# Half of the first feed-forward product by seven block products instead of eight

## The chip, the cores and the metric

The kernel runs on one core of a Trainium2 chip. The metric is the time that the device needs for one execution, in microseconds (us); the lower the better. The engines named here are TensorE (PE, matrix products; PEld is its weight load), VectorE (DVE), ScalarE (ACT), GpSimd (POOL) and SyncE (SP, which issues the loads). SBUF is the core's working memory, PSUM the eight banks of 128 x 512 fp32 into which PE adds up its products.

## The reference, cut to what matters

One encoder block on 256 tokens of width 2048, all in float32: a mixer of two branches (retention and latent attention), gated and merged, and then a feed-forward part of width 8192. The change touches the latter only:

```python
D_MODEL = 2048; SEQ = 256; D_FF = 4 * D_MODEL

h = h + _mixer(u, positions, ...)                # ends in  merged @ w_out
z = _rmsnorm(h, norm_mlp_g[l]) @ w_up[l]         # (256 x 2048) @ (2048 x 8192)
h = h + jnp.square(jax.nn.relu(z)) @ w_down[l]   # (256 x 8192) @ (8192 x 2048)
return _rmsnorm(h, norm_f_g)
```

## The kernel before

**Split products.** Every large product is made of fp32r products: an operand is split into `hi`, its value cast to fp32r, and `lo`, the rest, and `hi*hi + hi*lo + lo*hi` is summed in PSUM. `weights` (L146 to L153) does that for a weight tile: SP loads 512 KB into a `raw` buffer (L148), ACT casts it to `hi` (L151), DVE subtracts to get `lo` (L152). There are five `raw` buffers and four each of `hi` and `lo`. `split` (L214 on) does the same to activations. Since a weight is used for all 256 tokens only, each of them is loaded, split and used once, and the loads run all through the kernel.

**First product.** hT is the transposed and normalized h, kept as hi and lo in SBUF. `w_up` is cut into 64 units of 128 columns. A unit (`t_unit`, L170) loads and splits two half-weights of 128x1024, then PE runs 16 matmuls with a block of `hi` stationary and 512 columns moving, hi and lo of hT side by side (`t_pass1`, L159), and 16 with a block of `lo` stationary and the 256 columns of hT's hi (`t_pass2`, L163). `joined` (L204 to L212) adds the two halves of the bank: ACT copies one (L206), DVE adds (L207, tile `val`). DVE squares what is above zero into `hid` (L800), which stays in SBUF. The units take turns in the four PSUM banks of the pool behind `mmps`; the other four (`atps`) serve transposes here. The first two units are begun in halves, since the last quarter of hT (`mlp_turn(3)`) is transposed after their first half.

**Before and after it.** The w_out product (L770 to L779) ends the mixer, and `mlp_turn` (L757) makes hT of its result, a quarter at a time. The second product (`down`, L807, lines L814 to L816) has hid's halves stationary and 512 columns of w_down moving, in all eight PSUM banks, and the kernel ends in normalizing and storing the output.

**What sets the order.** All engines have queues of their own and work in order. The program is written in order of the data, and the framework's scheduler then orders each engine's instructions by a simulated timeline; the first loads and the last two units of the second product are held to the written order.

## Time and profile before

| what | value |
|---|---|
| median of 3 runs | 1631.94 us (1631.42 to 1632.12) |
| profiled execution | 1632.22 us, its span 1630.4 us |
| first product, from its first matmul to the first of the second product | 915.47 to 1272.66 us, 357.2 us |
| granted PE clock, mean | 0.998 |
| HBM read / written | 300.84 MB / 2.10 MB |

The profile comes from one execution. Busy time of an engine is what its instructions cover; PE's matmuls overlap, so their price is read from the distance of their starts, not from the duration given. "A <- B" in a wait means that A stood idle until B was done. Lines (L152) are those of the kernel before. Groups by line tell the name of the tile written, then those read: `lo<-raw,hi`, `z<-hT,hi`. Where a window is asked for (915:1273, in us from the start of the span), busy times are those inside it.

### The profile page before, as it was taken

The page shows a single profiled execution, that of the slowest core. Times are in us where ns is not written, and L with a number is a line of the kernel's source. Part 1 is how long each engine was busy: PE and PEld are TensorE (multiplying, and loading weights), DVE is VectorE, ACT ScalarE, POOL GpSimd, SP SyncE. Part 2 cuts the span into 40 slices and gives each one's busy share as a digit, 9 for nine tenths or more (in the row PEclk, how much of TensorE's full clock was granted, in tenths as well). Part 3 has the DMA queues.
Part 4 walks back from the last instruction along what each step waited for, and adds up shares of the span by engine and source line. Part 5 has one row for each costly group of instructions (what it writes and reads, how often), then busy time and mean ns, then how long its engine had stood idle before and what let it go on. Part 6 is the DMA issues. An engine that isn't in the chain of part 4 may idle for free.

```text
span 1630.4 us, 23041 instructions
## 1 busy us (share of the span) xinstructions
PE 1614.9 (99%) x8782; PEld 1398.8 (86%) x8782; DVE 996.2 (61%) x1491; ACT 809.7 (50%) x1249; POOL 49.5 (3%) x62
## 2 busy tenths in 40 slices
PE   8999999999999999999999999999999999999997
PEld 6888888888889889888888888888888888888886
DVE  7974588655556658666765555555555555555555
ACT  6544555544445556765545544444444444444444
POOL 7100000000000000000000000000000000000001
PEclk9999999999999999999999999999999999999999
DMA  8665544555556554325575555555555655555553
GB/s 306 200 233 193 187 156 166 169 192 186 190 170 203 190 191 146 125 94 176 186 246 187 174 193 188 192 189 186 191 192 184 223 194 192 193 193 195 192 194 112
DMA packets 84480, 304.46 MB, mean 187 GB/s; under 512 B 9360, under 2 KB 9488, under 8 KB 83600
## 3 DMA queue, kind: packets, MB, share of 16 engines
q1 hardware_dynamic: 84368, 302.98, 55.3%
q8 instruction: 69, 1.13, 0.3%
q14 instruction: 43, 0.35, 0.1%
HBM read 300.84 MB, written 2.10 MB: 186 GB/s over the span
## 4 chain that ended last, share of the span: by engine, by line
PE 97%; DVE 1%; issue 0%; DMA 0%; ACT 0%; POOL 0%; SPq 0%; DVEq 0%; POOLq 0%; ACTq 0%
PE z L159 14%; PE z L163 8%; PE dn L816 7%; PE dn L814 7%; PE dn L815 7%; PE rg L159 4%; PE yr L159 4%; PE gr L159 4%; PE gm L159 4%; PE mo L159 4%; PE qk L159 2%; PE gr L163 2%; PE yr L163 2%; PE gm L163 2%; PE rg L163 2%; PE mo L163 2%
## 5 line engine op out<-in xcount | busy, mean ns | idle before, releaser
L152 DVE TENSOR_TENSOR lo<-raw,hi 128x1024 fp32r<-128x1024 f32 (+2 forms) x562 | 666.0, 1204 | 521.6 <-ACT hi L151 248.3
L151 ACT CAST hi<-raw 128x1024 fp32r<-128x1024 f32 (+2 forms) x562 | 580.8, 1035 | 536.9 <-PE z L159 135.2
L159 PE MATMUL z<-hT,hi 128*128 128x512 f32 x1024 | 245.5, 391 | 0.0
L159 PEld LDWEIGHTS z<-hT,hi 128*128 128x128 f32 x1024 | 188.0, 188 | 36.1
L815 PE MATMUL dn<-lo,dh 128*128 128x512 f32 x512 | 199.2, 389 | 0.0
L816 PE MATMUL dn<-hi,dl 128*128 128x512 f32 x512 | 199.2, 389 | 0.0
L814 PE MATMUL dn<-hi,dh 128*128 128x512 f32 x512 | 198.9, 389 | 0.0
L163 PEld LDWEIGHTS z<-hT,lo 128*128 128x128 f32 x1024 | 131.6, 191 | 5.1
L163 PE MATMUL z<-hT,lo 128*128 128x256 f32 x1024 | 133.1, 283 | 0.0
L815 PEld LDWEIGHTS dn<-lo,dh 128*128 128x128 f32 x512 | 96.1, 188 | 20.1
L816 PEld LDWEIGHTS dn<-hi,dl 128*128 128x128 f32 x512 | 96.1, 188 | 19.9
L814 PEld LDWEIGHTS dn<-hi,dh 128*128 128x128 f32 x512 | 96.1, 188 | 19.8
L216 ACT CAST dh<-hid 128x256 fp32r<-128x256 f32 x64 | 26.0, 407 | 89.3 <-PE dn L815 89.3
L159 PE MATMUL mo<-my,hi 128*128 128x512 f32 x256 | 65.5, 396 | 0.4 <-DVE val L207 0.4
L159 PE MATMUL rg<-x,hi 128*128 128x512 f32 x256 | 64.0, 395 | 0.0
L159 PE MATMUL yr<-ry,hi 128*128 128x512 f32 x256 | 61.4, 391 | 0.0
L159 PE MATMUL gr<-x,hi 128*128 128x512 f32 x256 | 61.3, 391 | 0.0
L159 PE MATMUL gm<-x,hi 128*128 128x512 f32 x256 | 61.1, 391 | 0.0
L159 PEld LDWEIGHTS gm<-x,hi 128*128 128x128 f32 x256 | 47.0, 188 | 9.1
L159 PEld LDWEIGHTS gr<-x,hi 128*128 128x128 f32 x256 | 47.0, 188 | 9.0
L159 PEld LDWEIGHTS yr<-ry,hi 128*128 128x128 f32 x256 | 46.9, 188 | 9.0
L159 PEld LDWEIGHTS rg<-x,hi 128*128 128x128 f32 x256 | 46.2, 188 | 8.6
(271 smaller groups left out, 2239.1 us busy)
## 6 DMA issues: line engine op xcount, KB each, us to landing
raw<-w_up SPq DMA_DIRECT2D x128, 512.0 KB, 4.2
raw<-w_down SPq DMA_DIRECT2D x128, 512.0 KB, 4.3
raw<-w_rv SPq DMA_DIRECT2D x32, 512.0 KB, 4.5
raw<-w_rg SPq DMA_DIRECT2D x32, 512.0 KB, 4.5
raw<-w_gret SPq DMA_DIRECT2D x32, 512.0 KB, 4.3
raw<-w_ret_o SPq DMA_DIRECT2D x32, 512.0 KB, 4.6
raw<-w_gmla SPq DMA_DIRECT2D x32, 512.0 KB, 4.4
raw<-w_out SPq DMA_DIRECT2D x32, 512.0 KB, 3.7
```

Source lines behind the costliest of these rows:

```text
L151: SC.copy(hi, raw)
L152: V.tensor_tensor(out=lo, in0=raw, in1=hi.bitcast(F32), op=ALU.subtract)
L159: PE.matmul(out, w[0][:, k], x.both(k0 + k), start=start and k == 0, stop=False)
L163: PE.matmul(out[:, :S], w[1][:, k], x.hi(k0 + k), start=False, stop=stop and k == n - 1)
L216: SC.copy(hi, val)
L814: mm(PE.matmul(out, dh[:, ts], hi[:, ws], start=i == 0, stop=False))
L815: mm(PE.matmul(out, dh[:, ts], lo[:, ws], start=False, stop=False))
L816: mm(PE.matmul(out, dl[:, ts], hi[:, ws], start=False, stop=end))
```

## The change

The columns of w_up are parted in two halves. Columns 4096 to 8191 are 32 units as before. Columns 0 to 4095 are computed by block products in the manner of Strassen and Winograd, in four groups of 1024 columns. In a group the product is one of 2x2 blocks: two token halves (128), two halves of a pair of 128 rows of K, two column halves (512). A step (`s_step`, eight per group, 32 in all) takes 256 rows of K and loads 1 MB of weights in two parts into `sraw` buffers, of which there are four for the steps alone. DVE forms sums of the raw blocks (`fa`, `fb`), and seven products follow in place of eight, each three matmuls of 128x512 with activations stationary. Each product has a PSUM bank for a whole group, so seven of the eight banks are taken, four by `mmps` and three by `atps`; the units' banks all come from `atps`. After eight steps `s_end` puts the seven sums together with DVE, the result of 256 x 1024 is transposed by PE in four turns (`turn`) and written by `square`. The combinations of hT that the products need are made once (`Combos.make`, four calls; two within the w_out product, two at the start of the first product).

Relu and square are now on ACT, and `hid` goes to device memory with an ACT-issued DMA through two `hs` buffers; the second product reads it back in tiles `hl` of 256 KB. The residual `hn` is stored and reloaded (`keep`, `hn2`); others use its SBUF room in between. Steps and units alternate: three units first, begun in halves; 32 steps over the next 27 units, so five times two steps come in a row; two units last. The second product takes the tiles of the units (32 to 63) first. Some small tiles move to another pool.

```diff
+SU = 4
+SJ = KT // 2
+ST = SU * 1024 // P
+EARLY, LATE = 3, 2
...
+    PRODUCTS = ((3, 0, 0), (4, 0, 1), (2, 1, 0), (5, 1, 1), (6, 2, 0), (1, 2, 1), (7, 3, 0))
+
+    class Combos:
+        FORM = {2: 0, 5: 1, 6: 2, 4: 3}
+        RAW = {1: (1, 0), 3: (0, 1), 7: (1, 1)}
+
+        def __init__(self, name, pair):
+            self.name, self.pair, self.t = name, pair, []
+
+        def make(self, c):
+            if c % 2 == 0:
+                self.t.append(big(f"{self.name}{c // 2}", F32R, (P, KT // 4, 2, 4, P)))
+            x, q = wtile("raw", [P, 2, 2, 2, P]), wtile("raw", [P, 2, 4, P])
+            hi, lo = self.pair.span(4 * c, 4)
+            xs = x.rearrange("p j k t n -> p (j k) (t n)")
+            V.tensor_tensor(out=xs, in0=hi.bitcast(F32), in1=lo.bitcast(F32), op=ALU.add)
+            a11, a12, a21, a22 = (x[:, :, k, t] for t in range(2) for k in range(2))
+            a2, a5, a6, a4 = (q[:, :, f] for f in range(4))
+            V.tensor_tensor(out=a2, in0=a11, in1=a12, op=ALU.subtract)
+            V.tensor_tensor(out=a5, in0=a11, in1=a21, op=ALU.subtract)
+            V.tensor_tensor(out=a6, in0=a2, in1=a21, op=ALU.subtract)
+            V.tensor_tensor(out=a4, in0=a6, in1=a22, op=ALU.add)
+            o = self.t[-1][:, c % 2 * 2 : c % 2 * 2 + 2]
+            split(o[:, :, 0], o[:, :, 1], q)
+
+        def get(self, f, j):
+            if f in self.RAW:
+                k, t = self.RAW[f]
+                ts = slice(t * P, (t + 1) * P)
+                return self.pair.hi(2 * j + k, ts), self.pair.lo(2 * j + k, ts)
+            o = self.t[j // 4][:, j % 4]
+            return o[:, 0, self.FORM[f]], o[:, 1, self.FORM[f]]
+
+    def s_step(qs, src, x, j, between):
+        uid[0] += 1
+        ra, rb = (zp.tile([P, 2, 512], F32, tag="sraw", bufs=4, name=f"sraw{uid[0]}{i}") for i in range(2))
+        nc.sync.dma_start(ra, src[:, :2])
+        nc.sync.dma_start(rb, src[:, 2:])
+        fa, fb = (forms[:, 2 * (j % 2) + i] for i in range(2))
+        V.tensor_tensor(out=fa, in0=rb[:, 1:].to_broadcast([P, 2, 512]), in1=ra, op=ALU.add)
+        V.tensor_tensor(out=fb[:, 0], in0=fa[:, 0], in1=ra[:, 1], op=ALU.add)
+        V.tensor_tensor(out=fb[:, 1], in0=fb[:, 0], in1=rb[:, 0], op=ALU.add)
+        ws = []
+        for i, r in enumerate((ra, fa, fb, rb[:, :1])):
+            if i in (1, 2):
+                hi, lo = (
+                    zp.tile([P, 2, 512], F32R, tag=kind, bufs=4, name=f"{kind}{uid[0]}{i}") for kind in ("shi", "slo")
+                )
+            else:
+                hi, lo = (wtile(kind, [P, r.shape[1], 512]) for kind in ("hi", "lo"))
+            split(hi, lo, r)
+            ws.append((hi, lo))
+        for n, (f, i, o) in enumerate(PRODUCTS):
+            if n == 4:
+                between()
+            (ah, al), (hi, lo) = x.get(f, j), ws[i]
+            first, last = j == 0, j == SJ - 1
+            PE.matmul(qs[f], ah, hi[:, o], start=first, stop=False)
+            PE.matmul(qs[f], al, hi[:, o], start=False, stop=False)
+            PE.matmul(qs[f], ah, lo[:, o], start=False, stop=last)
+
+    def s_end(qs, out, tmp):
+        t3, e, f = (tmp[:, i] for i in range(3))
+        c11, c12, c21, c22 = (out[:, t, c] for t in range(2) for c in range(2))
+
+        def tt(o, a, b, op=ALU.add):
+            V.tensor_tensor(out=o, in0=a, in1=b, op=op)
+
+        SC.copy(t3, qs[3])
+        tt(e, qs[6], t3)
+        tt(f, qs[2], e, ALU.subtract)
+        tt(c21, qs[4], f)
+        tt(c11, qs[5], f)
+        tt(e, e, qs[5], ALU.subtract)
+        tt(c12, qs[1], e)
+        tt(c22, qs[7], t3)
...
+    zctx = ExitStack()
+    zp = zctx.enter_context(tc.tile_pool(name="zp", bufs=1))
+    hidd = ctx.enter_context(tc.tile_pool(name="hidd", bufs=1, space=bass.MemoryType.DRAM))
+    hc = Combos("hc", hT)
...
+        if c in (1, 2):
+            hc.make(c - 1)
...
-    up = [mmps(f"z{i}") for i in range(2)]
-    for i in range(2):
-        t_half(up[i], A["w_up"][i], hT, 0)
+    hid = [hidd.tile([P, 2, S], F32, name=f"hid{i}") for i in range(FT // 2)]
+    zo = big("zo", shape=(P, 2, 4, 512))
+
+    def square(pair, n, val):
+        t = zp.tile([P, 2, S], F32, tag="hs", bufs=2, name=f"hs{pair}{n}")[:, : val.shape[1]]
+        SC.activation(t, val, AF.Relu)
+        SC.activation(t, t, AF.Square)
+        SC.dma_start(hid[pair][:, n : n + val.shape[1]], t)
+
+    def s_units():
+        turns = []
+        for u in range(SU):
+            qs = {f: (mmps if f in (3, 4, 2, 5) else atps)(f"zs{u}{f}") for f in range(1, 8)}
+            for j in range(SJ):
+                s_step(qs, A["w_up_s"][u, j], hc, j, turns.pop(0) if turns and j else lambda: None)
+                yield
+            s_end(qs, zo[:, 0].rearrange("p (t c) n -> p t c n", t=2), zo[:, 1])
+
+            def turn(u, jj):
+                pT = atps(f"zt{u}{jj}")
+                for j in range(2):
+                    kt = 2 * jj + j
+                    for t in range(2):
+                        o = j * S + t * P
+                        src = zo[:, 0, 2 * t + kt // 4, kt % 4 * P : kt % 4 * P + P]
+                        PE.transpose(pT[:, o : o + P], src, ident)
+                square(4 * u + jj, 0, pT.rearrange("p (j n) -> p j n", j=2))
+
+            turns = [lambda u=u, jj=jj: turn(u, jj) for jj in range(4)]
+        for fn in turns:
+            yield
+            fn()
+
+    forms = None
+    steps = s_units()
+    early = [atps(f"z{i}") for i in range(EARLY)]
+    for i, pz in enumerate(early):
+        t_half(pz, A["w_up"][i], hT, 0)
         if i == 0:
             mlp_turn(3)
-    hid = [big(f"hid{i}") for i in range(3)]
-    hid.append(hp.tile([P, KT, S], F32, name="hid3"))
-    for i in range(FT):
-        if i < 2:
-            pz = up[i]
-            t_half(pz, A["w_up"][i], hT, 1)
-        else:
-            pz = mmps(f"z{i}")
-            t_unit(pz, A["w_up"][i], hT)
-        z = joined(pz)
-        V.scalar_tensor_tensor(hid[i // KT][:, i % KT], in0=z, scalar=0.0, in1=z, op0=ALU.max, op1=ALU.mult)
+            keep = hidd.tile([P, 2, D], F32, name="hnkeep")
+            SC.dma_start(keep, hn)
+            hc.make(2)
+            forms = big("forms", shape=(P, 4, 2, 512))
+    for i, pz in enumerate(early):
+        t_half(pz, A["w_up"][i], hT, 1)
+        square((ST + i) // 2, i % 2, joined(pz).unsqueeze(1))
+        if i == 0:
+            hc.make(3)
+    done = 0
+    for i in range(EARLY, FT - ST):
+        while done < SU * SJ and done * (FT - ST - EARLY - LATE) <= (i - EARLY) * SU * SJ:
+            next(steps)
+            done += 1
+        pz = atps(f"z{i}")
+        t_unit(pz, A["w_up"][i], hT)
+        square((ST + i) // 2, i % 2, joined(pz).unsqueeze(1))
+    for _ in steps:
+        pass
+    hn = big("hn2", shape=(P, 2, D))
+    nc.sync.dma_start(hn, keep)
+    zctx.close()
...
-    for i in range(FT):
+    for n, i in enumerate((*range(ST, FT), *range(ST))):
+        if n % 2 == 0:
+            hl = hp.tile([P, 2, S], F32, tag="hl", bufs=3, name=f"hl{i}")
+            nc.sync.dma_start(hl, hid[i // 2])
         dh = hp.tile([P, S], F32R, tag="dh", bufs=3, name=f"dh{i}")
         dl = hp.tile([P, S], F32R, tag="dl", bufs=3, name=f"dl{i}")
-        split(dh, dl, hid[i // KT][:, i % KT])
+        split(dh, dl, hl[:, i % 2])
         ws = []
         for half in range(2):
             w = weights(A["w_down"][i][:, half * 1024 : (half + 1) * 1024], [P, 1024])
             ws.append(w)
-            if i < FT - LAST:
+            if n < FT - LAST:
                 for t in range(2):
                     for c in (2 * half, 2 * half + 1):
-                        down(i, t, c, w, (dh, dl))
-        if i >= FT - LAST:
-            tail.append((i, ws, (dh, dl)))
+                        down(n, t, c, w, (dh, dl))
+        if n >= FT - LAST:
+            tail.append((n, ws, (dh, dl)))
...
+def _s_steps(w):
+    k, n = w.shape
+    b = w.reshape(k // 256, 2, P, n // 1024, 2, 512)
+    q = np.stack([b[:, 0, :, :, 1], b[:, 1, :, :, 0], b[:, 1, :, :, 1], b[:, 0, :, :, 0]], axis=3)
+    return np.ascontiguousarray(q.transpose(2, 0, 1, 3, 4))
```

More of the change, by code (lines that the diff above doesn't have):

```diff
@@ L30 @@
 FT = DFF // P
+SU = 4
+SJ = KT // 2
+ST = SU * 1024 // P
+EARLY, LATE = 3, 2
+SSF = 68
 EPS = 1e-6
@@ L231, in block_kernel @@
     SC.activation(warm, halfpi, AF.Copy)
-    cold = cp.tile([P, 512], BF16, name="cold")
+    rctx = ExitStack()
+    rope_pool = rctx.enter_context(tc.tile_pool(name="rope", bufs=2))
+    cold = rope_pool.tile([P, 512], BF16, tag="cold", bufs=1, name="cold")
     V.memset(cold, 0.0)
@@ L237, in block_kernel @@
         PE.matmul(spin, cold[:, :P], cold, start=True, stop=True)
-    rctx = ExitStack()
-    rope_pool = rctx.enter_context(tc.tile_pool(name="rope", bufs=2))
     ictx = ExitStack()
@@ L349, in block_kernel @@
         PE.matmul(pb[:, t * P : (t + 1) * P], rr[:, t], ident, start=True, stop=True)
-    rxb = cp.tile([P, S], F32, name="rxb")
+    rxb = rope_pool.tile([P, S], F32, tag="rxb", bufs=1, name="rxb")
     V.tensor_copy(rxb, pb[:, :S])
@@ L357, in table @@
         sgn = vec[:, V_INV + 2 + j : V_INV + 3 + j]
-        own = ip if j == 0 else cp
-        cos = own.tile([P, S], F32, name=f"cos{j}")
-        sin = own.tile([P, S], F32, name=f"sin{j}")
+        cos, sin = (
+            (ip if j == 0 else rope_pool).tile([P, S], F32, tag=f"{name}{j}", bufs=1, name=f"{name}{j}")
+            for name in ("cos", "sin")
+        )
         tc.keep_in_program_order(SC.activation(sin, ang, AF.Sin, scale=sgn))
@@ L520, in block_kernel @@
         cc = big("cc", F32R, shape=(P, 2 * LT, 2, S))
-        kpe = cp.tile([P, S], F32, name="kpe")
+        kpe = rope_pool.tile([P, S], F32, tag="kpe", bufs=1, name="kpe")
         lp = ExitStack()
@@ L802, in block_kernel @@
+    for _ in steps:
[3 more added lines that the diff above has]
+    zctx.close()
+    jp = ctx.enter_context(tc.tile_pool(name="jp", bufs=1))
     pd = [[(mmps if t == 0 else atps)(f"dn{t}{c}") for c in range(4)] for t in range(2)]
-    ssf = cp.tile([P, 2, 68], F32, name="ssf")
+    ssf = cp.tile([P, 2, SSF], F32, name="ssf")
     rf = cp.tile([P, 2], F32, name="rf")
@@ L843, in finish @@
         V.scalar_tensor_tensor(h, in0=ps, scalar=rh2[:, t : t + 1], in1=h, op0=ALU.mult, op1=ALU.add)
-        junk = hp.tile([P, 512], F32, tag="junk", bufs=2, name=f"junk{t}{n}")
+        junk = jp.tile([P, 512], F32, tag="junk", bufs=2, name=f"junk{t}{n}")
         SC.activation(junk[:, lo:hi], h, AF.Square, accum_out=ssf[:, t, n : n + 1])
@@ L931 @@
         "w_out": _n_units(np.asarray(w_out)[0]),
-        "w_up": _t_units(np.asarray(w_up)[0]),
+        "w_up_s": _s_steps(np.asarray(w_up)[0][:, : SU * 1024]),
+        "w_up": _t_units(np.asarray(w_up)[0][:, SU * 1024 :]),
         "w_down": np.ascontiguousarray(np.asarray(w_down)[0].reshape(FT, P, D)),
@@ L935 @@
     }
-    nc = bacc.Bacc("TRN2", target_bir_lowering=False, num_devices=1)
+    nc = bacc.Bacc("TRN2", target_bir_lowering=False, num_devices=1, dynamic_dma_scratch_size=2048)
     A = {
```

## The prediction

> **What bounds the kernel now.** I read the page from the top: busy time, then the chain of waits, then stages by window.

> ```profile
> PE 1614.9 (99%) x8782; PEld 1398.8 (86%) x8782; DVE 996.2 (61%) x1491; ACT 809.7 (50%) x1249; POOL 49.5 (3%) x62
> PE 97%; DVE 1%; issue 0%; DMA 0%; ACT 0%; POOL 0%; SPq 0%; DVEq 0%; POOLq 0%; ACTq 0%
> ```

> PE is never without work, and the chain is PE's own. The change sits in the first feed-forward product, so I cut out that stage (915 to 1273) and its neighbours:

> ```profile
> core 0: us, PE busy (x) PEld busy (x) DVE busy (x) ACT busy (x) POOL busy (x), PEclk, DMA share, GB/s
> 832.00:915.00 83.00, 83.00 (x379) 68.68 (x378) 45.21 (x49) 38.96 (x53) 0.00 (x0) 1.00 0.59 201
> 915.00:1273.00 358.00, 358.00 (x2061) 316.22 (x2060) 203.05 (x267) 162.66 (x204) 0.00 (x0) 1.00 0.56 189
> 1276.00:1610.00 334.00, 334.00 (x1476) 276.54 (x1475) 176.54 (x184) 148.05 (x184) 0.00 (x0) 1.00 0.57 191
> ```

> In 358 us PE has no gap; DVE works 203 and ACT 163. Who is early shows in the waits of the stage: the splitters wait for PE to free their buffers, never for a load.

> ```profile
> DVE lo L152 <- PE z L163: 142.1, 60, 2.4
> ACT hi L151 <- PE z L159: 133.7, 121, 1.5
> ```

> So PE's work is what the stage costs, and DVE has some 149 us of slack in it. PE's prices come from the timeline, of one unit and of the second product:

> ```profile
> 1005.46 3.82 PE L159 MATMUL z<-hT,hi 128*128 128x512 f32 x16
> 1009.11 2.08 PE L163 MATMUL z<-hT,lo 128*128 128x256 f32 x16
> 1011.03 0.40 PE L159 MATMUL z<-hT,hi 128*128 128x512 f32 x1
> ...
> 1272.66 0.40 PE L814 MATMUL dn<-hi,dh 128*128 128x512 f32 x1
> ...
> 1289.91 0.39 PE L815 MATMUL dn<-lo,dh 128*128 128x512 f32 x1
> ```

> A unit takes 1011.03−1005.46 = 5.57 us. The second product's matmul has the form that the steps will have (activations stationary, 512 weight columns moving): 76 from 1272.66 to 1289.91, 0.227 us each.

> **What leaves PE.** The stage was 357.2 us (first z matmul 915.47, first dn 1272.66). 32 units stay: 178.1. The other 32 become 32 steps of 7 products x 3 matmuls: 21 x 0.227 = 4.77 us each, 152.7. Added: 64 transposes of the result, 128x128; such transposes in the trace of before start 0.07 to 0.09 us apart, 5.8 in all. With the four old transposes' 1.3 the sum is 337.9: PE's saving is 19.3 us, and 1613 is the floor.

> **What comes to DVE.** This is the price that decides. Rows of before: a 128x1024 subtraction 1.22 us, 1.14 from start to start when queued behind each other (59.12 to 60.26); 128x512 0.69, at most some 0.62 queued; 128x256 0.42, 0.34 queued.

> - A step builds sums of raw weights (one 1024, two 512) and splits seven operands of 512 columns where a unit splits four (three instructions of 1024, one of 512): 4 x 1.22 + 3 x 0.69 = 6.95 us, 6.4 queued. Two loads' splits in a unit were 2.45.
> - A unit keeps two splits and the join: 2.87, 2.62 queued; its relu-square leaves DVE for ACT.
> - Four ends of seven 512s: 4.8 each, 4.3 queued. Two of the four activation combinations (add 1024, four 256, subtract 1024: 4.1 each, 3.7 queued) fall here; the other two into the w_out stage, where DVE has 83−45 = 38 us of cover.

> Sum in the stage: 32 x 6.95 + 32 x 2.87 + 4 x 4.8 + 2 x 4.1 + 1.7 (hT splits) = 343 us at full durations, 318 queued. PE needs 338. DVE goes from 57% to level with PE: the cover that the splits had is gone.

> ACT: per step 3 casts of 1024 (1.05) and one 512 (0.62), 3.8; per unit two casts, join 0.37, two 256 functions 0.41, 3.3; ends, turns and combinations about 25. Some 250 of 357: not the bound, but four of its results per step stand ahead of DVE.

> **DMA and queues.** Bytes per step equal a unit's (1 MB). A raw load is issued by SP behind the split that frees its buffer and lands 3.0 to 7.2 us later, median 4.3:

> ```profile
> L148 SPq DMA_DIRECT2D raw<-w_up x116: 327/328/1140, 932.8 to 1250.9; - x116
> ...
> DMA to landing us min/median/max: 3.0/4.3/7.2
> ```

> Unit loads still have five buffers and, in the order of the program, some 15 us or more of DVE work ahead of their use, but for the last few. The steps' four buffers hold only two steps: between the release of the last one and the sum that needs it, the order leaves DVE 1.9 to 7.9 us of other work, about 5 at the median, and nothing at step 11, 1.9 at step 27, 2.3 to 3.1 at 14, 19 and 24. Against issue 0.33 + landing 4.3 these shortfalls add up to some 22 us of DVE waiting, part of it inside time in which DVE would have waited for PE anyway. 8.4 MB of hid are written and read back, and 4 MB for hn: the stage's DMA share was 0.56 at 189 GB/s for about 67 MB, so 12 MB more here (and 8 in the next product, 0.57) fit below 0.7. The read-backs (256 KB, 2.5 us by the output's row) are issued by SP with three buffers, one per two down units (11 us): hidden. The reload of hn (2 MB, 8.8 us by hn's load) waits for a matmul of step 27 on SP and stands ahead of the loads of steps 30 and 31; they can come up to 4 us late. Relu-square on ACT writes through two buffers, freed when their write has landed (2 to 4 us): the next one can hold ACT for 1 to 2 us at the turns.

> **PSUM.** Seven of eight banks now hold the seven sums of a group of eight steps. A unit, formerly one of four banks in rotation, has the eighth alone: its first matmul waits for the DVE join of the previous unit, and so do the transposed turns, whose bank ACT frees. The joins stand in DVE's queue among the steps' splits. Walking the programs of PE, DVE and SP with the durations above, PE stands still:

> - at the start (turns and three units in the bank ring): 3.4
> - first group's end: DVE has nearly 14 us queued (two steps' splits and the end's seven ops) before the join of unit 8, about 5.6 late for PE; then step 11's load, 3.4 more: 9.0
> - turns of group 0 between units 11 and 14: 3
> - ends of groups 1 and 2: 2 each; double step with two turns at units 18 to 20: 1.6; double step, turns and hn reload at 24 to 28: 5.5
> - the last turns, and the change to the second product: 2

> Together 28.5. In the plain stretches (one unit, one step: PE 10.34, DVE 9.0 to 9.8) PE holds its pace, so I add nothing there. Ends: a stall of zero everywhere gives −19.3; DVE at full durations with all load waits 343 + 22 gives the upper end, below. I take 28.5, since the waits are in the order itself.

> **Sum.** −19.3 + 28.5 = +9.2 on the profiled execution's 1632.2 (span 1630.4; it is the median's 1631.9 within 0.3) = 1641. The second product and all before 832 stay.

> **Rivals.**
> *PE stays the bound (faster).* Loads that take 3.0 us rather than 4.3, or DVE catching up during the plain stretches, would leave only the group ends and the turns: 10 to 15 us of stalls, 1623 to 1628. For it: the queued rates, DVE's 318 against 338. Against: one bank for units. It decides at 19.3 us of stalls in all: below that the kernel is faster.
> *DVE is the bound all through.* If steps' operations depend on each other and pay full durations, 343 + the 22 of load waits + 8 in which DVE starts or ends without work = 373 to 380: 1648 to 1655, to 1660 with landings near the 7.2 maximum.
> *Loss and gain cancel.* Stalls of 16 to 23: within 1629 to 1635.
> *The clock drops in the gaps.* At the program's start PE stands idle for 8 to 10 us and the granted clock then shows 0.69 in 10–14 us and 0.92 in 14–20, a loss of 4 x 0.31 + 6 x 0.08 = 1.7 us. If each of the four longest waits did that, +7: 1648. All other windows read 1.00, as there is no gap in them.

> [...]

> **How the numbers follow.** 0.2% (3.3 us) is what can be told from no change. Chances: the forecast's case (1636 to 1648) 0.42, DVE bound 0.22, clock 0.06, cancelling 0.10, faster 0.20. The likeliest one's own range is 1636 to 1648. The whole range goes from 1622, which takes in the faster rival, to 1660.

> **What would show it.** Right: DVE over 90% busy in the stage, PE's idle time ended by join (val) on DVE and, for DVE, by the steps' loads; the longest PE gap at the first group's end; 21 matmuls of a step 4.8 us apart. Wrong: PE idle below 19 us in the stage, DVE waiting on PE for its hi and lo buffers in most steps; or DVE's 512 operations from PSUM above 0.8 us, which moves it up.

## The result, and the profile after

The changed kernel takes 1651.63 us (median of 4 runs, 1648.99 to 1655.33) against 1631.72 for the kernel before beside it: 1.0124 times, 95% interval 1.0101 to 1.0146, that is 19.9 us slower. The forecast was 1641. The sign and the whole range (1622 to 1660) hold; the likeliest case's own range (1636 to 1648) does not, and the forecast change of 9.2 us is less than half of what was measured.

The profiled execution took 1649.97 us (span 1648.2, granted clock 0.994), 17.8 more than that of before. The stage, from the first z matmul to the first dn matmul, runs from 914.2 to 1288.5: 374.3 us in place of 357.2, so 17.1 more; it begins 1.2 earlier, and from its end to the end of the span there are 2.0 more. Engine totals, and the windows that answer to those of before:

```profile
PE 1610.6 (98%) x8494; PEld 1374.4 (83%) x8494; DVE 1119.6 (68%) x1607; ACT 889.7 (54%) x1385; POOL 49.8 (3%) x62
```

```profile
832.00:914.00 82.00, 82.00 (x374) 67.72 (x373) 54.56 (x66) 41.72 (x56) 0.00 (x0) 1.00 0.53 184
914.00:1291.00 377.00, 354.49 (x1777) 294.37 (x1776) 318.80 (x368) 236.96 (x331) 0.00 (x0) 0.98 0.63 214
1291.00:1625.00 334.00, 333.38 (x1471) 274.96 (x1470) 174.88 (x183) 150.51 (x189) 0.00 (x0) 1.00 0.64 215
```

In the stage (second line) PE now has 22.5 us without work, and its clock is 0.98, where it was 1.00. DVE went from 203 to 319 us, ACT from 163 to 237. DVE is 85% busy, not the over 90% that was forecast. What it and PE waited for, in the waits of the changed kernel:

```profile
DVE forms L248 <- DMA sraw<-w_up_s: 25.6, 16, 4.8
...
PEld zs L268 <- DVE lo L299: 7.3, 5, 3.0
...
PEld z L164 <- ACT hs L879: 7.0, 6, 2.0
...
PEld zs L268 <- DVE slo L299: 5.7, 9, 1.0
```

DVE, which waited for no load in this stage before, waits 25.6 us at the first sum of a step (`forms`, L248) for the step's raw weights. PE waits for splits of DVE, and its units for the bank that a turn's relu (`hs`) still reads. Of the 22.4 us in which PE stands idle in the stage, 11.1 end with a split for a step (`lo`, `slo`, `shi`), 4.7 with a turn's relu, 2.7 with a unit's join (`val`), and 2.3 with the copy at a group's end (`zo`). The chain of waits shows how the one becomes the other, at the end of the first group:

```profile
1004.03 5.36 DMA sraw<-w_up_s
1009.48 1.22 DVE forms L248
1010.78 0.98 issue
1011.76 1.22 DVE lo L157
1012.97 0.60 DVE forms L249
1013.58 1.14 DVE lo L157
1014.71 1.74 DVE lo L299 x2
1016.45 1.14 DVE slo L299
1017.59 0.34 DVE val L289
1018.07 5.68 PE z L164 x16
1023.74 1.90 PE z L168 x16
```

A load lands 5.4 us after it could be issued; the sum stands first in DVE's queue, and behind it stand the splits and the join (`val`) for which PE's next unit waits. Then the unit's first 16 matmuls take 5.68 us instead of 3.63: the clock has fallen. By windows of 10 us:

```profile
1004.00:1014.00 10.00, 7.07 (x38) 5.54 (x36) 8.27 (x10) 6.76 (x9) 0.00 (x0) 1.00 0.40 132
1014.00:1024.00 10.00, 6.73 (x21) 5.13 (x22) 7.60 (x11) 3.16 (x5) 0.00 (x0) 0.66 0.65 223
1024.00:1034.00 10.00, 10.00 (x52) 8.53 (x52) 10.00 (x13) 6.73 (x9) 0.00 (x0) 1.00 0.32 102
```

The trace has such half-speed stretches at three places of the stage (967, 1015 and 1165), of 3.41, 6.83 and 3.41 us. Matmuls that ran inside them took 5.8 us longer than at full speed.

### The profile page after: what moved, and what is told of

It is laid out like the page before. It is cut to its first block, busy times and chain, and to the rows that moved or that the text cites. A ratio compares the mean times of both kernels' runs of the same rounds, so it can differ in the third digit from the quotient of the medians.

```text
span 1648.2 us, 22846 instructions
## 1 busy us (share of the span) xinstructions
PE 1610.6 (98%) x8494; PEld 1374.4 (83%) x8494; DVE 1119.6 (68%) x1607; ACT 889.7 (54%) x1385; POOL 49.8 (3%) x62
## 5 line engine op out<-in xcount | busy, mean ns | idle before, releaser
L157 DVE TENSOR_TENSOR lo<-raw,hi 128x1024 fp32r<-128x1024 f32 (+2 forms) x498 | 590.7, 1202 | 382.8 <-ACT hi L156 245.4
L156 ACT CAST hi<-raw 128x1024 fp32r<-128x1024 f32 (+2 forms) x498 | 511.9, 1032 | 423.6 <-PE dn L952 95.4
L164 PE MATMUL z<-hT,hi 128*128 128x512 f32 x512 | 127.8, 401 | 8.6 <-ACT hs L879 4.7
L164 PEld LDWEIGHTS z<-hT,hi 128*128 128x128 f32 x512 | 97.5, 194 | 32.7 <-ACT hs L879 7.0
L952 PEld LDWEIGHTS dn<-hi,dl 128*128 128x128 f32 x512 | 96.1, 188 | 19.9
L299 DVE TENSOR_TENSOR slo<-forms,shi 128x1024 fp32r<-128x1024 f32 x64 | 77.9, 1221 | 6.8 <-ACT shi L298 6.8
L298 ACT CAST shi<-forms 128x1024 fp32r<-128x1024 f32 x64 | 66.9, 1048 | 28.8 <-DVE forms L248 21.1
L298 ACT CAST hi<-sraw 128x1024 fp32r<-128x1024 f32 x64 | 53.3, 835 | 31.8 <-PE z L164 23.0
L168 PEld LDWEIGHTS z<-hT,lo 128*128 128x128 f32 x512 | 66.1, 191 | 2.8
L168 PE MATMUL z<-hT,lo 128*128 128x256 f32 x512 | 67.1, 283 | 0.0
L299 DVE TENSOR_TENSOR lo<-sraw,hi 128x1024 fp32r<-128x1024 f32 x64 | 59.4, 953 | 7.4 <-PE z L168 3.5
```

What stands on the lines that cost most here:

```text
L156: SC.copy(hi, raw)
L157: V.tensor_tensor(out=lo, in0=raw, in1=hi.bitcast(F32), op=ALU.subtract)
L164: PE.matmul(out, w[0][:, k], x.both(k0 + k), start=start and k == 0, stop=False)
L168: PE.matmul(out[:, :S], w[1][:, k], x.hi(k0 + k), start=False, stop=stop and k == n - 1)
L298: SC.copy(hi, val)
L299: V.tensor_tensor(out=lo, in0=val, in1=hi.bitcast(F32), op=ALU.subtract)
```

## The experiments

There are four theories. By A, PE's stalls come from all that stands in DVE's queue, and the clock's half-speed windows come on top. By B, the waits for raw weights are the cause. By C, DVE's sum of work is the bound. By D, the one bank of the units is the cause. Times are medians; the kernel before took 1631.3 to 1631.8 us beside them. In brackets stands the ratio to it, with its 95% interval. Where a run leaves something out, its text says what. In the runs of the changed kernel the scheduler laid out the engines' queues anew after each edit, so none of them changes one thing alone.

**Steps without loads.** Only two steps' weights are loaded; the rest use them again, so the result is not the product.

```diff
+    kept = []
...
-        ra, rb = (zp.tile([P, 2, 512], F32, tag="sraw", bufs=4, name=f"sraw{uid[0]}{i}") for i in range(2))
-        nc.sync.dma_start(ra, src[:, :2])
-        nc.sync.dma_start(rb, src[:, 2:])
+        if len(kept) < 2:
+            ra, rb = (zp.tile([P, 2, 512], F32, tag="sraw", bufs=4, name=f"sraw{uid[0]}{i}") for i in range(2))
+            nc.sync.dma_start(ra, src[:, :2])
+            nc.sync.dma_start(rb, src[:, 2:])
+            kept.append((ra, rb))
+        ra, rb = kept[j % 2]
```

> Left out: only the first two steps load their raw weights, the other 30 use those again (sums, splits and matmuls are all done). So no step waits for a load. Theory A (PE's stalls come from everything that stands in DVE's queue, and the half-speed windows of the clock come on top): DVE's 25.6 us of waiting for raw step weights goes, but a good half of it had run beside PE's work; stage 374 to about 360, time 1634 to 1640. Theory B (the two-step raw buffers are the cause): nearly all 25 us come back, 1622 to 1628. Theory C (DVE's sum of work is the bound): at most 5 us, 1645 or more.

1635.09 (1.0024 of before, 1.0014 to 1.0033): 16.5 us less than the changed kernel, at the lower end of A and above B's range. The stage is 359.5 us, still 2.3 longer than before the change. So without the loads' waits the larger part of the loss goes, but not all.

**Steps without sums.** The sums of raw blocks are made in the first two steps only; the other steps use those.

```diff
-        V.tensor_tensor(out=fa, in0=rb[:, 1:].to_broadcast([P, 2, 512]), in1=ra, op=ALU.add)
...
+        if len(made) < 2:
+            V.tensor_tensor(out=fa, in0=rb[:, 1:].to_broadcast([P, 2, 512]), in1=ra, op=ALU.add)
...
+            made.append(j)
```

> Left out: the sums of raw blocks are made in the first two steps only, later steps split those again; loads, splits and matmuls stay. DVE loses 30 x (1.22 + 2 x 0.69) = 78 us of its 319 in the stage. Theory C: stage down to PE's 338 and some 10, time about 1622 to 1628. Theory B: the loads are now waited for by DVE with less work ahead of them, no more than 5 us gained, 1645 or more. Theory A: 10 to 15 us, 1635 to 1641.

1624.31 (0.9959, 0.9944 to 0.9974): 27 us less, inside C's range. But this edit takes away two things at once: some 70 us of DVE's work (248 us in the stage in place of 318), and the one instruction that waited for the loads first. DVE's load waits are gone from its trace. It doesn't tell C from B.

**A second bank for the units.** The seventh product is added into the sixth's bank, so the steps' result is not the product; all work is done.

```diff
-            first, last = j == 0, j == SJ - 1
+            first, last = j == 0 and f != 7, j == SJ - 1 and f != 1
...
-            qs = {f: (mmps if f in (3, 4, 2, 5) else atps)(f"zs{u}{f}") for f in range(1, 8)}
+            qs = {f: (mmps if f in (3, 4, 2, 5) else atps)(f"zs{u}{f}") for f in range(1, 7)}
+            qs[7] = qs[1]
```

> Left out: the seventh product is added into the sixth's PSUM bank, so two banks are free for units and turns instead of one (the result of the steps is not the product; every load, sum, split and matmul is done). Theory D (the one bank of the units is the cause): PE's waits before a unit (val and hs, some 13 us) go, time 1635 to 1640. Theories B and C: under 4 us, 1647 or more. Theory A: 4 to 8 us.

1623.98 (0.9954, 0.9939 to 0.9969): 27.7 us less, over twice of D's own price. In its waits the loads count 11.4 us in place of 25.6: the scheduler had also ordered DVE's queue anew. So this too was two things, and it is taken up again below.

**More raw buffers.** Six for four, and four `hs` for two; the pool `hp` is opened after the stage to make room.

```diff
-        ra, rb = (zp.tile([P, 2, 512], F32, tag="sraw", bufs=4, name=f"sraw{uid[0]}{i}") for i in range(2))
+        ra, rb = (zp.tile([P, 2, 512], F32, tag="sraw", bufs=6, name=f"sraw{uid[0]}{i}") for i in range(2))
...
-    hp = ctx.enter_context(tc.tile_pool(name="hp", bufs=1))
+    zq = ctx.enter_context(tc.tile_pool(name="zq", bufs=1))
...
-        t = zp.tile([P, 2, S], F32, tag="hs", bufs=2, name=f"hs{pair}{n}")[:, : val.shape[1]]
+        t = zq.tile([P, 2, S], F32, tag="hs", bufs=4, name=f"hs{pair}{n}")[:, : val.shape[1]]
...
     zctx.close()
+    hp = ctx.enter_context(tc.tile_pool(name="hp", bufs=1))
```

> Nothing left out: six raw buffers for the steps (three steps) instead of four, and four for what goes to device memory instead of two; the second product's pool is opened later to make the room. Theory B: DVE's waits for raw step weights almost vanish, 20 us gained, 1628 to 1634. Theory A: 8 to 14 us, 1637 to 1643. Theory C: under 4 us.

1647.55 (1.0100, 1.0083 to 1.0117), only 4.1 us less, which is not clear of the noise, as the two intervals overlap. The waits have not gone, they have grown:

```profile
DVE forms L248 <- DMA sraw<-w_up_s: 29.8, 16, 3.5
```

The order of DVE's instructions says why. With a third step's buffers the scheduler had put each first sum further ahead: between the release of a step's second buffer and the use of its next load there stand again 1.2 to 7.4 us of DVE's work (by the durations of the trace), 4.8 at the middle, against 4.4 with four. On the chip a load takes 4.6 us at the median and up to 12.0. Why the scheduler put the sums so early no run shows. DVE, which works in order, waits at the sum while work stands behind it. B in the form "too few buffers" falls; what is left of it is "the sum's place in the queue".

**The sums later in the queue.** The same four buffers; the first sum of a step may not be issued on DVE before the last split of the step before it.

```diff
-        V.tensor_tensor(out=fa, in0=rb[:, 1:].to_broadcast([P, 2, 512]), in1=ra, op=ALU.add)
+        with tc.issue_after(tail_lo[-1].ins) if tail_lo else ExitStack():
+            V.tensor_tensor(out=fa, in0=rb[:, 1:].to_broadcast([P, 2, 512]), in1=ra, op=ALU.add)
...
-            split(hi, lo, r)
+            tail_lo.append(split(hi, lo, r))
```

> Nothing left out, same buffers: only the first sum of a step is queued on DVE behind the last split of the step before, so that at least 6 us of DVE work stand between the release of a raw buffer and the use of its next load. If the waits for loads come from the place of the sums in DVE's queue, and not from the number of buffers, they go from 25.6 us to under 5, and as without the loads some 12 to 16 us come back: 1635 to 1641. If DVE's lateness has other causes: 1647 or more. If the later sums make PE wait in turn: slower than 1652.

1628.22 (0.9981, 0.9971 to 0.9990): 23.4 us less than the changed kernel with no work taken away, more than the 12 to 16 expected, and 0.2% faster than before. Between the release of a step's second buffer and the use of its next load there now stand 6.1 to 12.4 us of DVE's work, 9.8 at the middle. Of the loads' waits on DVE 0.8 us are left, and in the stage (351.3 us; window below) DVE has 315 us of work, nearly the 318 of the changed kernel, while PE's clock is back at 1.00:

```profile
DVE forms L251 <- DMA sraw<-w_up_s: 0.8, 1, 0.8
```

```profile
914.10:1265.40 351.30, 342.01 (x1764) 289.76 (x1764) 315.34 (x367) 231.78 (x327) 0.00 (x0) 1.00 0.69 228
```

So the place of the sums is a cause of the loss, and an order without these waits makes up for all of it. The edge is the only edit, but PE's order came out different too: units that twice stand directly in a row in the stage now have two matmuls of steps between them. How much of the 23.4 us is due to such moves was not parted from the loads' waits. The kernel also beats the run without loads (1635.09), in which DVE had another order again; what held that one up was not followed.

**Half banks.** A unit adds up in 256 columns, so its bank holds two units; turns use the same halves.

```diff
...
+        for n, (w, hi, lo) in enumerate(mms):
+            with behind() if n == 0 else ExitStack():
+                PE.matmul(out, w, hi, start=n == 0, stop=False)
+            PE.matmul(out, w, lo, start=False, stop=False)
...
-        square((ST + i) // 2, i % 2, joined(pz).unsqueeze(1))
+        square((ST + i) // 2, i % 2, pz.unsqueeze(1))
```

> Nothing left out: a unit adds up in 256 columns (48 matmuls of 256 in place of 16 of 512 and 16 of 256), so that its bank holds two units, one being written while the other is read, and no join is needed; the turns use the same halves. PE's work grows by 32 x (48 x 0.12 - 5.57) = 6 us. If the one bank is what couples PE to DVE's queue, 27 - 6 = 21 us come back, a few more by DVE's 32 joins less: 1626 to 1632. If the gain with two banks came from elsewhere: 1645 or more.

1656.03 (1.0148, 1.0133 to 1.0163), a miss: slower than the changed kernel. The stage did shorten (362.1 us), but from its end to the end of the span there are 376.4 us in place of 359.7. The last turns, now eight halves, come after the second product has begun, and PE waits there for relu and the device writes behind it, 3.10 us in one gap; the two transposes after it take 0.68 us, the two before it 0.44 (PE's timeline):

```profile
1299.77 0.44 PE L899 MATMUL zz<-con,zo 128*128 128x128 f32 x2 [0.47 <-ACT hs L879]
1303.31 0.68 PE L899 MATMUL zz<-con,zo 128*128 128x128 f32 x2 [3.10 <-ACT hs L879]
```

The run says little of the bank, as it brought a new wait.

**Half banks and the order.** Both edits, to the half banks' kernel:

```diff
-        V.tensor_tensor(out=fa, in0=rb[:, 1:].to_broadcast([P, 2, 512]), in1=ra, op=ALU.add)
+        with tc.issue_after(tail_lo[-1].ins) if tail_lo else ExitStack():
+            V.tensor_tensor(out=fa, in0=rb[:, 1:].to_broadcast([P, 2, 512]), in1=ra, op=ALU.add)
```

> Nothing left out: both edits together. If the loads' waits and the bank are separate causes: 8 to 12 us less than with the half banks alone, 1615 to 1623. If the bank is only the way by which late splits reach PE, the second edit adds less than 4 us.

1641.53 (1.0064, 1.0048 to 1.0080): 14.5 us under the half banks alone, above the forecast time by the same tail (stage 351.2, the rest 376.6). So the order's gain shows in another kernel too.

**Gaps in the kernel before.** At every fourth unit the bank of the unit before is used again, which was to make 15 waits of some 2.5 us.

```diff
-            pz = mmps(f"z{i}")
+            if i % 4:
+                pz = mmps(f"z{i}")
             t_unit(pz, A["w_up"][i], hT)
+        if (i + 1) % 4 == 0:
+            for _ in range(2):
+                SC.copy(pz, pz)
```

> The kernel before, nothing left out, with 15 waits put into PE's work: at every fourth unit of the first product the bank of the unit before is used again, after two copies in place and the join (about 0.25 + 2 x 0.7 + 0.4 + 0.5 = 2.5 us). If gaps of this size cost only their length: 15 x 2.5 = 38, 1670, clock 0.998 as before. If a gap of 2 to 3 us can bring a half-speed window of 3.4 us: up to 15 x 1.7 = 26 us more, 1675 to 1696, clock 0.98 to 0.99. [...]

1631.33 (0.9999, 0.9989 to 1.0008): no gap of PE appears in its trace, so it priced nothing. PE had other units' matmuls to run.

**One bank for all units of the kernel before.** Now PE has nothing else to run while it waits.

```diff
-            pz = mmps(f"z{i}")
             t_unit(pz, A["w_up"][i], hT)
+        if i >= 2:
+            for _ in range((i - 2) // 20):
+                SC.copy(pz, pz)
         z = joined(pz)
```

> The kernel before, nothing left out, but all units of the first product add up in one PSUM bank, so PE waits after each for copy and join: some 1.1 us after units 2 to 21, 1.75 after units 22 to 41 (one more copy in place on ACT first), 2.45 after units 42 to 61 (two). The sum of the gaps is 112 us: 1744 at a granted clock of 0.998. [...] If a gap of 2 to 3 us can bring a half-speed window of 3.4 us: 1.00 in the first third, below it in the last one, up to 20 x 1.7 = 34 us more, 1760 to 1780.

1825.27 (1.1188, 1.1166 to 1.1211), granted clock 0.967: 194 us slower, not 112. Two units of PE's timeline (in brackets the idle time before):

```profile
946.40 3.92 PE L159 MATMUL z<-hT,hi 128*128 128x512 f32 x16 [1.89 <-DVE val L207]
950.16 2.07 PE L163 MATMUL z<-hT,lo 128*128 128x256 f32 x16
954.12 5.54 PE L159 MATMUL z<-hT,hi 128*128 128x512 f32 x16 [1.89 <-DVE val L207]
```

PE stands idle for 1.89 us per unit in the first two thirds, not 1.1, and the copies changed it little (2.18 in the last third), so the three sizes asked for were not made. DVE's queue says why. Two `lo` splits wait for matmuls at the unit's end; the second one (1.22 us) stands before the join and ends long after the copy (timeline, 951.9 to 954.3 us):

```profile
951.37 2.36 DVE L152 TENSOR_TENSOR lo<-raw,hi 128x1024 fp32r<-128x1024 f32 x2 [4.56 <-PE z L163]
952.32 0.37 ACT L206 COPY join<-z 128x256 f32<-128x256 f32 x1 [0.87 <-PE z L163]
953.65 0.42 DVE L207 TENSOR_TENSOR val<-z,join 128x256 f32<-128x256 f32 x1
```

The question of the clock is answered all the same: after a gap of 1.89 us, at about every second unit, 16 matmuls take 5.54 us in place of 3.92. The granted clock is 0.90 from 930 to 1080 us, 0.90 to 1250 and 0.87 to 1440: 15 + 17 + 25 = 57 us lost. The gaps, start to start, sum up to 132: together 189 of the 194.

**Two banks, with the order.** To the kernel with the later sums; the steps' result again is not the product.

```diff
+            first, last = j == 0 and f != 7, j == SJ - 1 and f != 1
...
+            qs[7] = qs[1]
```

> Left out: the seventh product is added into the sixth's bank (two free banks for units and turns), and the first sums of the steps are queued on DVE as in the run with that edit alone. If the bank is a cause of its own: 8 us or more below the 1628.2 of the order alone, 1612 to 1620. If the second bank had helped only because the planner's order had shorter waits for loads with it: 1621 to 1628.

1615.35 (0.9902, 0.9887 to 0.9917): 12.9 us below the order alone. So the one bank costs time also where the loads' waits are gone. Taken the other way round, the second bank alone brought 27.7 us and the order on top of it 8.6. Each of the two makes up for the whole loss; they overlap, and together they bring 36.3. The stage is 340.2 us, where the forecast's sum of PE's work was 337.9, and PE is idle for 1.4:

```profile
914.80:1255.00 340.20, 338.82 (x1764) 290.26 (x1763) 315.26 (x367) 229.88 (x327) 0.00 (x0) 1.00 0.71 235
```

DVE does the same 315 us here, 93% of the stage, and holds PE up no longer: C falls. What is left is A, in which the place of the sums and the one bank both have a part.

**More buffers, with the order.** To the kernel with the later sums, the edits of the run with more raw buffers:

```diff
+        ra, rb = (zp.tile([P, 2, 512], F32, tag="sraw", bufs=6, name=f"sraw{uid[0]}{i}") for i in range(2))
...
+        t = zq.tile([P, 2, S], F32, tag="hs", bufs=4, name=f"hs{pair}{n}")[:, : val.shape[1]]
```

> Nothing left out: six raw buffers for the steps, four for what goes to device memory, and the first sums queued as before in that edit. The loads are already early enough with four, so these buffers add nothing; the four others take the waits on device writes (4.1 us on ACT): 1624 to 1628. If the depth of the raw buffers counts once the order is right: below 1622.

1620.77 (0.9936, 0.9921 to 0.9951): 7.5 us below the order alone, and 10.5 below the kernel before. Nothing is left out, so this version beats both. The time falls where the depth of the raw buffers was to count; but as the buffers on the way to device memory changed with them, which of the two brought it was not parted. The stage is 346.0 us:

```profile
915.60:1261.60 346.00, 341.30 (x1765) 289.84 (x1765) 315.92 (x367) 232.13 (x327) 0.00 (x0) 1.00 0.69 229
```

**Three groups in place of four.** That kernel with 24 steps and 40 units.

```diff
-SU = 4
+SU = 3
```

> Nothing left out: the same with three groups of steps in place of four (24 steps, 40 units). PE's floor rises by 8 x 0.79 - 16 x 0.09 = 4.9 us, DVE's work falls by some 8 x (6.95 - 2.87) + 4.8 = 37 us of 319 and one group end less. If DVE's load still makes PE wait: 1618 to 1625, below the four groups. If the four groups' waits were all of the order: 1626 to 1632.

1637.93 (1.0041, 1.0026 to 1.0055), a miss: 17 us slower than with four, where both guesses were 1618 to 1632. DVE has 282 us of work in place of 316, and it does not help. PE is idle in the stage for 12.4 us in place of 4.7. With more units than steps two units often come in a row, and the second waits for the first one's join; this line was not among the waits of the kernel with four groups:

```profile
PEld z L164 <- DVE val L292: 11.3, 13, 1.3
```

## Why the prediction was right or wrong

**The bound and PE's floor: right.** Steps' matmuls start 0.227 us apart; with two banks and the order the stage came to 340.2 us, 2.3 over the 337.9 reckoned.

**DVE's work: right, at its lower end.** 319 us measured (914 to 1291), 318 to 343 reckoned: the queued rates hold. The forecast's queued terms add up to 315 rather than 318.

**Stalls by place: right in sum, by luck in part.** Measured from the distance of starts (less 0.227 for a matmul of 512 columns, 0.12 for 256, 0.075 for a transpose), summed where over 0.3 us and the clock taken off:

| place | forecast | measured |
|---|---|---|
| start | 3.4 | 2.1 |
| double step at 965 | none | 2.0 |
| first group's end | 9.0 | 6.7 |
| turns of group 0 | 3 | 3.6 |
| second group's end | 2 | 2.0 |
| double step with turns, 1158 | 1.6 | 4.5 |
| third group's end | 2 | 1.8 |
| units 24 to 28 | 5.5 | 3.6 |
| change to the second product | 2 | 2.0 |
| sum | 28.5 | 28.3 |

By place the errors are up to 2.9 us, +5.5 and -5.7 in all, and cancel. Nor is the way to PE the forecast one: PE's idle time was to end with joins, and only 2.7 of 22.4 us do; half of it ends with splits for the steps.

**The plain stretches: a term that failed, by some 4 us.** "PE holds its pace, so I add nothing there": waits of 0.1 to 0.3 us each, left out of the table, sum up to 4.4.

**The clock: the other term that failed.** It stood in the sum with nothing, as a rival with a chance of 0.06 that priced it at 7. The half-speed windows cost 5.8 us in the profiled execution. PE's work at the distances above is 19.4 us less than before, so the terms give −19.4 + 28.3 + 4.4 + 5.8 − 1.2 (the earlier start) = 17.9, against 17.8 measured and 9.2 forecast. The two terms put at nothing are what the forecast lacks. The median lies 1.7 above that execution, and there the clock is lower: the four runs are 1648.99 and 1649.97 at 0.994, 1653.29 at 0.991, 1655.33 at 0.990. With six buffers alone the four runs do not fall into that order (1644.55 at 0.993, 1646.23 at 0.997), so the share of the clock in the 19.9 is known for the profiled execution only. The rival took its loss from the program's start, where PE's longest gap is 3.3 us (7.69 to 11.01); the stage has half speed at three places, and no single gap there is longer than 2.6 us.

**The cause: named, but put too low.** The forecast counted 22 us of DVE waiting for loads (25.6 measured) and let it reach PE by name at the first group's end alone, with 3.4 us (and near the end through the reload of `hn`), laying the rest to DVE's backlog and the bank. The later place of the sums took 23.4 us off, more than the whole loss. A sum that waits in DVE's queue holds up the splits and joins behind it, as the chain at the first group's end shows; whether each stall of the table came about so was not followed. The bank, which the forecast held for the main thing, is not cleared: it is worth 27.7 us with the sums where they were and 12.9 with the sums later. That raw buffers for two steps are too few was not said but lay near; more of them alone bring 4.1 us, which is not clear of the noise.

**Rivals.** "DVE is the bound all through" fell, though the measured time lies in its range of 1648 to 1655: with two banks DVE does 315 us in a stage of 340 and holds PE up no longer. The side that decides, stalls under 19.3 us, is where five of these kernels came out, three of which leave something out.

## What to carry to other kernels

When an engine works in order and a scheduler placed its instructions ahead of time, ask of each instruction that waits for a load who stands behind it. Here more buffers did not help while the order used them up; pinning the instruction behind work that was needed sooner did, and then more buffers helped too. Where a change opens gaps in TensorE's work, price them with the clock: gaps of 1.89 us (the one-bank run), or two of 0.53 and 1.60 us within 3.4 us (the changed kernel, before 1165), cost here up to 1.7 us on top of their length. And a saving on one engine is paid by the buffers between it and the others: here the product's seven banks left one to the units, which cost 12.9 us even with the better order.

## What the runs showed of the hardware

In the run with one bank, where the gaps are 1.89 us, 16 matmuls took 5.53 us in place of 3.92 at every second unit of the timelines read. These units begin 17.04 to 17.05 us apart (1090.96 and 1108.01; 1237.03, 1254.08 and 1271.12). The granted clock from 1080 to 1097 and from 1097 to 1114 us is 0.90: 1.7 us lost in each, which is what half speed over 3.41 us comes to. With gaps of 2.18 us such units begin 17.62, 9.65, 17.64 and 9.62 us apart (1380.46 to 1434.99).

In the runs without sums and with a second bank, gaps of 0.57 and 1.16 us, with transposes between them, were followed by eight matmuls that took 3.41 and 3.16 us in place of 2.09. In the kernel with the order alone a gap of 1.63 us was followed by 16 matmuls in 3.92 us; PE is idle for 9.3 us of its stage, and the clock there is 1.00.

The way from a unit's last matmul over an ACT copy (0.37) and a DVE add (0.42) to the next matmul in the same bank took 1.89 us in the one-bank run. Some 1.0 of it is DVE's queue: the copy was done at 952.69, and the add began at 953.65, behind a split. In the unit at 1398 us, with two copies in place ahead, it took 2.18.
